# The closing norm of the last 256 rows, partly on the matmul array: one decoder layer step on one Trainium2 core

## The chip, the core and the metric

The kernel runs on one core of a Trainium2 chip, in one launch. The metric is the device time of one execution in microseconds; before the change it is 1931.59 us (the median of three runs, 1929.88 to 1933.46). Engines are named as in the profile: PE is the matmul engine (its weight loads are shown as PEld), DVE the vector engine, ACT the scalar engine, POOL the fourth compute engine, and SP the queue that issues nearly all DMAs here.

## The reference, cut to what matters

One layer of a hybrid decoder is computed in fp32 for 512 prompt rows (with 16 learned rows ahead of them) and 8 sample rows. The change lies in the last statement, the closing layer norm of the prompt rows:

```
def layer_norm(x, g, b):
    mu = jnp.mean(xf, -1, keepdims=True)
    var = jnp.mean(jnp.square(xf - mu), -1, keepdims=True)
    return (xf - mu) * lax.rsqrt(var + LN_EPS) * g + b
...
    ff = jnp.einsum('btf,fd->btd', a, w_down)
    return layer_norm(DEEPNORM_ALPHA * h1 + ff, ln2_g, ln2_b)
```

With r = 1/sqrt(var + eps), a row's result is r·(x·g) + (−mu·r)·g + b. The second form is the one that the changed kernel uses for six of its eight pieces.

## The kernel before

The trunk keeps features on partitions and tokens along the free axis. Each fp32 product is made of three fp32r matmuls: a weight is split into a high part (ACT, line 187) and a low part (DVE, line 188), the activations likewise, and `products` issues high·high (line 203), high·low (204) and low·high (206).

The end of the program is the part that matters. The down projection keeps 16 accumulators `acc[m]`, one for each 128 output features, over 520 token columns (8 sample, 512 prompt). Its last share, of four blocks of the inner dimension, is done by `down(h, m)`: for half h of the tokens (h = 0: the samples and prompt rows 0 to 255; h = 1: prompt rows 256 to 511) and block m, PE does four times three products of 256 columns into a bank of PSUM (the tiles `d0_m` and `d1_m`; `d` in the profile), and DVE adds the bank to `acc[m]` (line 1333). The weights are loaded by SP in four groups (line 1325) and split during h = 0; h = 1 uses the splits again.

The closing norm needs rows on partitions. So once four blocks of a half are added, PE transposes 128 rows by 512 features (tiles `tz8` and `tz136` for the first half, `tz264` and `tz392` for the second; line 1347), ACT copies them out of PSUM to a tile `z` (line 1349), and DVE takes statistics (line 1351). When all four quarters of a row block are there, `Rows.end` makes mean and reciprocal deviation by a chain of tiny operations (lines 236 to 250) and passes twice over each 512-wide quarter: centre and scale by the weight row (line 1358), then multiply by r and add the bias row (line 1360), and SP writes the quarter out (line 1361). Two row blocks make eight quarters, hence sixteen DVE passes of 128x512. Those of the first half are handed out piecewise among the products of h = 1 by the generator `ends`; those of the second half come after all products.

`sample_rows` does the same norm for the eight sample rows with features on partitions, in steps that the loop calls in turn (lines 1391 to 1408, the last of them a transposition `to` and sixteen small writes).

The order on each engine is set by a scheduler that places instructions by its own estimate of times; within an engine they run strictly in that order, and each waits on semaphores of other engines. `step(engine)` pins a written order.

## Time and profile before

| | |
|---|---|
| runs shown | 1933.46, 1929.88, 1931.59 us; median 1931.59 |
| profiled execution: span from first to last instruction | 1931.1 us |
| PE busy over the span | 1894.4 us (98%) |
| DVE busy | 1539.9 us (80%) |
| ACT busy | 944.1 us (49%) |
| span after the last product of the down projection (issued at 1911.33) | 19.8 us |

The page's span leaves out what lies ahead of the first and behind the last instruction; it stands 0.5 us below the median of the runs shown. In timeline rows the first number is the start in us, the second the time that the group of instructions covers, then engine, source line, operation, output and inputs, shape and count; a bracket gives idle time before the group and who ended it. In a table of windows each engine has busy time and the number of instructions, and PEclk is the granted clock of PE (1.00 is full). Successive DVE or PE instructions overlap slightly in these rows, so a cost is taken from start to start.

### The profile page before, as it was taken

The numbers are of one execution on the slowest core, as the hardware profiler recorded it, in microseconds if no ns is written. First come the engines' busy times: TensorE is split into PE (matmuls) and PEld (weight loads), VectorE is DVE, ScalarE is ACT, GpSimd is POOL, SyncE is SP. The second block draws the span as 40 slices with busy tenths as digits, with TensorE's granted clock in tenths as the row PEclk, the third lists the DMA queues.
The fourth block names the chain that finished last, engine by engine and source line by source line (L and its number), as shares of the span: only waits on it lengthen the run. The fifth ranks groups of instructions, "written<-read, shape, count | busy, mean of one in ns | idle before, by whom it ended". The sixth has DMA issues, their size and how long they took to land.

```text
span 1931.1 us, 39334 instructions
## 1 busy us (share of the span) xinstructions
PE 1894.4 (98%) x15533; PEld 1865.8 (97%) x15533; DVE 1539.9 (80%) x2734; ACT 944.1 (49%) x1808; POOL 2.7 (0%) x9
## 2 busy tenths in 40 slices
PE   9999999999999999999999999999999999999996
PEld 8999999999989999999999999999999999999996
DVE  6666667768777888888888888888877888888878
ACT  6644445545654544554455555555554444344341
POOL 0000000000000000000000000000000000000000
PEclk9999999999999999999999999999999999999998
DMA  8732222665744555454545445454469664645332
GB/s 276 233 101 66 71 78 75 211 202 193 250 150 164 160 160 172 142 162 158 175 139 178 141 138 165 146 167 145 164 212 356 214 221 162 223 163 202 94 99 89
DMA packets 145241, 319.28 MB, mean 165 GB/s; under 512 B 14288, under 2 KB 66232, under 8 KB 144952
## 3 DMA queue, kind: packets, MB, share of 16 engines
q1 hardware_dynamic: 144480, 315.71, 49.7%
q8 instruction: 122, 2.00, 0.4%
q10 hardware_dynamic: 576, 1.05, 0.2%
q14 instruction: 63, 0.52, 0.1%
HBM read 265.22 MB, written 54.03 MB: 165 GB/s over the span
## 4 chain that ended last, share of the span: by engine, by line
PE 92%; DVE 4%; ACT 2%; DMA 1%; issue 1%; SPq 0%; DVEq 0%; ACTq 0%
PE p_g L203 7%; PE p_g L204 7%; PE p_g L206 7%; PE p_u L203 7%; PE p_u L206 7%; PE p_u L204 7%; PE tri L203 7%; PE tri L206 7%; PE tri L204 7%; PE o L203 3%; PE o L206 3%; PE o L204 3%; PE p_u L996 2%; PE mm_u L203 2%; PE mm_u L206 2%; PE mm_u L204 2%
## 5 line engine op out<-in xcount | busy, mean ns | idle before, releaser
L187 ACT CAST rr<-fr 128x512 fp32r<-128x512 f32 (+1 forms) x1056 | 658.0, 643 | 776.6 <-DVE fr L196 224.0
L188 DVE TENSOR_TENSOR rr<-fr,rr 128x512 fp32r<-128x512 f32 (+1 forms) x1056 | 738.0, 717 | 264.5 <-ACT rr L187 253.2
L196 DVE TENSOR_TENSOR fr<-fr 128x1024 f32<-128x1024 f32 (+1 forms) x304 | 319.7, 1052 | 5.8 <-DMA fr<-in_w_g_dram 5.0
L203 PE MATMUL p_g<-rr 128*128 128x260 f32 x830 | 235.5, 285 | 7.4 <-ACT rr L187 7.1
L206 PE MATMUL p_g<-rr 128*128 128x260 f32 x830 | 230.6, 282 | 0.0
L204 PE MATMUL p_g<-rr 128*128 128x260 f32 x788 | 221.8, 282 | 0.0
L203 PE MATMUL p_u<-rr 128*128 128x260 f32 x770 | 217.5, 283 | 0.2 <-ACT rr L187 0.2
L206 PE MATMUL p_u<-rr 128*128 128x260 f32 x770 | 215.3, 282 | 0.0
L204 PE MATMUL p_u<-rr 128*128 128x260 f32 x748 | 210.6, 282 | 0.0
L206 PE MATMUL tri<-rr 128*128 128x260 f32 x696 | 196.8, 283 | 1.5 <-DVE rr L188 1.5
L203 PE MATMUL tri<-rr 128*128 128x260 f32 x696 | 197.0, 283 | 0.7 <-ACT rr L187 0.7
L204 PE MATMUL tri<-rr 128*128 128x260 f32 x696 | 196.7, 283 | 0.0
L203 PEld LDWEIGHTS p_g<-rr 128*128 128x128 f32 x830 | 156.2, 188 | 9.9 <-ACT rr L187 9.4
L206 PEld LDWEIGHTS p_g<-rr 128*128 128x128 f32 x830 | 155.2, 189 | 0.0
L204 PEld LDWEIGHTS p_g<-rr 128*128 128x128 f32 x788 | 148.1, 188 | 0.0
L203 PE MATMUL o<-rr 128*128 128x260 f32 x512 | 145.0, 284 | 0.3 <-ACT rr L187 0.3
L203 PEld LDWEIGHTS p_u<-rr 128*128 128x128 f32 x770 | 144.9, 188 | 0.3 <-ACT rr L187 0.3
L206 PEld LDWEIGHTS p_u<-rr 128*128 128x128 f32 x770 | 144.6, 189 | 0.0
L204 PE MATMUL o<-rr 128*128 128x260 f32 x512 | 144.1, 282 | 0.0
L206 PE MATMUL o<-rr 128*128 128x260 f32 x512 | 143.6, 282 | 0.2 <-DVE rr L188 0.2
L204 PEld LDWEIGHTS p_u<-rr 128*128 128x128 f32 x748 | 140.6, 188 | 0.0
L206 PEld LDWEIGHTS tri<-rr 128*128 128x128 f32 x696 | 131.3, 189 | 2.2 <-DVE rr L188 2.2
(320 smaller groups left out, 4570.0 us busy)
## 6 DMA issues: line engine op xcount, KB each, us to landing
fr<-in_w_u_dram SPq DMA_DIRECT2D x100, 512.0 KB
fr<-in_w_g_dram SPq DMA_DIRECT2D x90, 512.0 KB
fr<-in_w_d_dram SPq DMA_DIRECT2D x64, 640.0 KB
t_d<-fr SPq DMA_DIRECT2D x140, 260.0 KB
fr<-in_w_o_dram SPq DMA_DIRECT2D x64, 512.0 KB
fr<-in_w_in_dram SPq DMA_DIRECT2D x48, 512.0 KB
rr<-t_d SPq DMA_DIRECT2D x87, 260.0 KB
mid_b<-t_d SPq DMA_DIRECT2D x53, 260.0 KB
```

The lines of the kernel that those rows point to most:

```text
L187: nc.scalar.copy(wh, s)
L188: last_lo[0] = (lo or nc.vector).tensor_sub(wl, s, wh.bitcast(F32)).ins
L196: i = op(*args).ins
L203: nc.tensor.matmul(o, wh, hi[j], start=first, stop=False, skip_group_check=onto)
L204: nc.tensor.matmul(o, wh, lo[j], start=False, stop=False, skip_group_check=onto)
L206: nc.tensor.matmul(o, wl, hi[j], start=False, stop=last, skip_group_check=onto)
L996: nc.tensor.matmul(bk, self.q(0, n - 1)[:, k * P:(k + 1) * P], z1[0][4 * (n - 1) + k // 2][:, k % 2, :], start=(k == 0), stop=(k == 7))
```

## The change

Lines after 1333 shift (the bank add becomes line 1335; `Rows.end` has 1360 and 1362). Four things change, all in the second half's norm and what stands around it.

First, the rows 256 to 511 are no longer `Rows` but a class `Last`. Its `turn(m-1)` transposes one block for both row blocks inside `down(1, m)`, after three quarters of its products; before, the transpositions of four blocks stood together behind every fourth `down`. Each full quarter of the first three is copied out and measured as before, and DVE then multiplies it by the weight row at once (`scale`, line 1434), before the mean is known.

Second, the fourth quarter stays in PSUM. Its statistics are taken in two pieces of 256 columns (line 1426); after the last one, DVE centres and scales it straight from PSUM (line 1450) and finishes it as before (line 1457).

Third, for the other six pieces (three quarters, two row blocks) the terms (−mu·r)·g + b are made by PE: three columns −mu·r and two of ones (tile `five`) are transposed (line 1480), split into a high and a low part (`lh`, `lw`), and multiplied with five prepared rows that hold the weight and bias in high and low parts (`rows5`), 512 columns at a time into a bank `sh` (line 1501). For three pieces DVE adds r times the scaled tile to the bank (line 1507). For the three others PE also multiplies the scaled tile by a diagonal matrix of r, in fp32 (line 1496; the diagonals are made by ACT, line 1484), and ACT copies the bank out (line 1504).

Fourth, `rows5` is prepared during h = 0: four times two small loads by SP, a rounding copy by ACT (line 1536) and a DVE pass of 5x512 (line 1537). The steps of `sample_rows` move to behind blocks 3, 7 and 11 of the second half, where they were behind 4, 10 and 15.

```diff
-    def down(h, m):
+    def down(h, m, mid=None):
 ...
         for f in range(4):
             products([out], wh[:, f, :], wl[:, f, :], [ah[f][:, hs]], [al_[f][:, hs]], f == 0, f == 3)
+            if f == 2 and mid:
+                mid()
         nc.vector.tensor_add(acc[m][:, hs], acc[m][:, hs], out)
 ...
+        def turn(self, m):
+            q, i = divmod(m, 4)
+            if i == 0:
+                self.tp = bank(f"tz{self.c0}_{q}", 512)
+            nc.tensor.transpose(self.tp[:, i * P:(i + 1) * P], acc[m][:, self.c0:self.c0 + P], ident)
+            if q == 3:
+                if i % 2:
+                    nc.vector.bn_stats(self.st[:, 3 + i // 2, :], self.tp[:, (i - 1) * P:(i + 1) * P])
+            elif i == 3:
+                z = zp.tile([P, 512], F32, tag="z", name=f"z{self.c0}_{q}", bufs=NZ)
+                nc.scalar.copy(z, self.tp)
+                nc.vector.bn_stats(self.st[:, q, :], z)
+                self.z.append(z)
+        def scale(self, q):
+            nc.vector.tensor_mul(self.z[q], self.z[q], gb[0][q])
 ...
+        def centre(x):
+            dve.scalar_tensor_tensor(zl[x.i], x.tp, mu[:, x.i:x.i + 1], gb[0][3], op0=ALU.subtract, op1=ALU.mult)
 ...
+        affine(part[0])
+        with step(dve):
+            dve.scalar_tensor_tensor(five[:, :, 0:3], wide(mu), -1.0, wide(r), op0=ALU.mult, op1=ALU.mult)
+        with step(dve):
+            centre(part[1])
+        affine(part[1])
 ...
+        def diag(n):
+            x, q = pieces[n]
+            with step(nc.tensor):
+                nc.tensor.matmul(bk[n], dg[x.i], x.z[q], start=True, stop=False, skip_group_check=True)
+        def shift(n):
+            x, q = pieces[n]
+            with step(nc.tensor):
+                nc.tensor.matmul(bk[n], lw[:, x.i * P:(x.i + 1) * P], rows5[:, q * 512:(q + 1) * 512], start=n > 2,
+                                 stop=True, skip_group_check=True)
+            if n < 3:
+                nc.scalar.copy(x.z[q], bk[n])
+            else:
+                with step(dve):
+                    dve.scalar_tensor_tensor(x.z[q], x.z[q], r[:, x.i:x.i + 1], bk[n], op0=ALU.mult, op1=ALU.add)
+            put_out(x, q, x.z[q])
+        diag(0)
+        diag(1)
+        for n in (3, 4, 5, 0, 1):
+            shift(n)
+        diag(2)
+        shift(2)
 ...
+        if m in (6, 8, 10, 12):
+            affine_rows(m // 2 - 3)
 ...
+    ends = chain.from_iterable([x.end() for x in rows])
+    for m in range(KT):
+        down(1, m, lambda: [x.turn(m - 1) for x in last if m])
+        for _ in range(2 if m % 4 == 1 else 1):
+            next(ends, None)
+        if m % 4 == 2 and m > 2:
+            for x in last:
+                x.scale(m // 4 - 1)
+        if m in (3, 7, 11):
+            next(sample)
```

Where the instructions end up is shown at three places. In the names, `d1_m` is the bank of block m in the second half, `tz264_q` and `tz392_q` the transposed quarters q of its two row blocks, `mid_c` holds the tiles z, and `fr` the accumulators and the rows of weight and bias.

On DVE, in the middle of the second half, around the eight bias passes of the first half's rows; before:

```order
L242 TENSOR_TENSOR fr_60<-fr_60 128x1 x2
L1360 SCALAR_TENSOR_TENSOR mid_c_20115<-mid_c_20115,fr_60 128x512 x5
L1333 TENSOR_TENSOR fr_60<-fr_60,d1_9_20659 128x256
L1360 SCALAR_TENSOR_TENSOR mid_c_20115<-mid_c_20115,fr_60 128x512 x3
L1351 BN_STATS fr_60<-mid_c_20115 128x6 x2
L1333 TENSOR_TENSOR fr_60<-fr_60,d1_10_20676 128x256
```

and now:

```order
L1434 TENSOR_TENSOR mid_c_20115<-mid_c_20115,fr_60 128x512
L242 TENSOR_TENSOR fr_60<-fr_60 128x1 x2
L1335 TENSOR_TENSOR fr_60<-fr_60,d1_7_20641 128x256
L1393 TENSOR_REDUCE fr_60<-zv_20659 128x8
L1362 SCALAR_TENSOR_TENSOR mid_c_20115<-mid_c_20115,fr_60 128x512 x8
L236 TENSOR_SCALAR fr_60<-fr_60 128x8
L1335 TENSOR_TENSOR fr_60<-fr_60,d1_8_20672 128x256
L1335 TENSOR_TENSOR fr_60<-fr_60,d1_9_20693 128x256
L1430 BN_STATS fr_60<-mid_c_20115 128x6 x2
```

The eight passes now stand in one piece, and the adds of blocks 8 and 9 behind them; before, block 8 was added ahead of them and block 9 between them.

On PE, where the third quarter of the second half is first transposed; before:

```order
L204 MATMUL d1_11_20705<-rr_61 128x256
L206 MATMUL d1_11_20705<-rr_61 128x256
L1347 MATMUL tz264_2_20720<-fr_60 128x128
L1347 MATMUL tz392_2_20727<-fr_60 128x128
L203 MATMUL d1_12_20770<-rr_61 128x256
```

and now:

```order
L204 MATMUL d1_9_20693<-rr_61 128x256
L206 MATMUL d1_9_20693<-rr_61 128x256
L1423 MATMUL tz264_1_20603<-fr_60 128x128
L1423 MATMUL tz392_1_20605<-fr_60 128x128
L1423 MATMUL tz264_2_20703<-fr_60 128x128
L1423 MATMUL tz392_2_20705<-fr_60 128x128
L203 MATMUL d1_10_20714<-rr_61 128x256
```

The pair that reads block 8 stood behind the products of block 11 and stands now behind those of block 9.

At the end, PE had only the transposition `to` left after the last transpositions of the rows; it now has

```order
L1423 MATMUL tz392_3_20804<-fr_60 128x128
L1480 MATMUL five_20866<-fr_60 5x128 x2
L1496 MATMUL sh0_0_20873<-mid_c_20115,fr_60 128x512
L1496 MATMUL sh1_0_20874<-mid_c_20115,fr_60 128x512
L1501 MATMUL sh1_1_20876<-rr_61 128x512
L1501 MATMUL sh0_2_20877<-rr_61 128x512
L1501 MATMUL sh1_2_20878<-rr_61 128x512
L1501 MATMUL sh0_0_20873<-rr_61 128x512
L1501 MATMUL sh1_0_20874<-rr_61 128x512
L1496 MATMUL sh0_1_20875<-mid_c_20115,fr_60 128x512
L1501 MATMUL sh0_1_20875<-rr_61 128x512
```

so two of the three diagonal products stand ahead of all the rank products, and the third behind five of them; `sh0` and `sh1` are the two row blocks.

More of the change, by code (lines that the diff above doesn't have):

```diff
@@ L49 @@
 NG = 56
-NZ = 19
+NZ = 16
 FRW, RRW, MDW = 18960, 24368, 9880
@@ L1409, in sample_rows, with __init__ @@
         yield
+    class Last:
+        def __init__(self, c0, i, dst):
+            self.c0, self.i, self.dst, self.z = c0, i, dst, []
+            self.st = pb.tile([P, 5, 6], F32, name=f"st_z{c0}")
+        def turn(self, m):
[13 more added lines that the diff above has]
+            nc.vector.tensor_mul(self.z[q], self.z[q], gb[0][q])
@@ L1411, in hybrid_step @@
     sample = sample_rows()
     next(sample)
-    rows = [Rows(NS + P * i, P, yp[P * i:P * (i + 1), :]) for i in range(4)]
-    for h, part in ((0, rows[:2]), (1, rows[2:])):
-        for m in range(KT):
-            down(h, m)
-            if h == 1:
-                for _ in range(2 if m % 4 == 1 else 1):
-                    next(ends, None)
-            if h == 0 and m in (1, 2):
-                for i, q in gb_loads[4 * m - 4:4 * m]:
-                    nc.sync.dma_start(gb[i][q], ln2gb[i:i + 1, q * 512:(q + 1) * 512].to_broadcast([P, 512]))
-            if m % 4 == 3:
-                for x in part:
-                    x.part(m // 4)
-            if (h, m) in ((0, 4), (0, KT - 1), (1, 4), (1, 10), (1, KT - 1)):
-                next(sample)
-        ends = chain.from_iterable([x.end() for x in part])
@@ L1430, in hybrid_step @@
-    for _ in ends:
-        pass
+    five = pb.tile([P, 2, 5], F32, name="five")
+    nc.gpsimd.memset(five, 1.0)
+    nident = pb.tile([P, 8], F32, name="nident")
+    nc.scalar.activation(nident, ident[:, 0:8], AF.Copy, scale=-1.0)
+    mask = pb.tile([P, 1], F32, name="mask")
+    nc.vector.tensor_add(mask, nident[:, 1:2], nident[:, 4:5])
+    lp = Pool(rr)
+    lh = lp.tile([5, 2 * P], F32R, name="lh")
+    lw = lp.tile([5, 2 * P], F32R, name="lw")
+    rows5 = lp.tile([5, D], F32R, name="rows5")
@@ new lines, in affine_rows @@
+    def affine_rows(q):
+        sl = slice(q * 512, (q + 1) * 512)
+        g5 = pb.tile([5, 512], F32, name="g5", bufs=1)
+        h5 = lp.tile([5, 512], F32R, name="h5", bufs=1)
+        nc.sync.dma_start(g5[0:3], ln2gb[0:1, sl].to_broadcast([3, 512]))
+        nc.sync.dma_start(g5[3:5], ln2gb[1:2, sl].to_broadcast([2, 512]))
+        nc.scalar.copy(h5, g5)
+        nc.vector.scalar_tensor_tensor(rows5[:, sl], h5.bitcast(F32), mask[:5], g5, op0=ALU.mult, op1=ALU.add)
+    rows = [Rows(NS + P * i, P, yp[P * i:P * (i + 1), :]) for i in range(2)]
@@ new lines, in hybrid_step @@
+    last = [Last(NS + P * i, i - 2, yp[P * i:P * (i + 1), :]) for i in (2, 3)]
+    for m in range(KT):
+        down(0, m)
+        if m in (1, 2):
+            for i, q in gb_loads[4 * m - 4:4 * m]:
+                nc.sync.dma_start(gb[i][q], ln2gb[i:i + 1, q * 512:(q + 1) * 512].to_broadcast([P, 512]))
+        if m in (6, 8, 10, 12):
+            affine_rows(m // 2 - 3)
+        if m % 4 == 3:
+            for x in rows:
+                x.part(m // 4)
+        if m in (4, KT - 1):
+            next(sample)
@@ L1435, in _layout @@
+    ends = chain.from_iterable([x.end() for x in rows])
+    for m in range(KT):
+        down(1, m, lambda: [x.turn(m - 1) for x in last if m])
[5 more added lines that the diff above has]
+        if m in (3, 7, 11):
+            next(sample)
+    for _ in chain(ends, sample):
+        pass
+    for x in last:
+        x.turn(KT - 1)
+    last_rows(last)
 def _layout(i):
```

40 lines of the change are left out of this document (added).

## The prediction

> **What bounds the kernel now.** I looked first at where the end is decided, with a table of windows over the last 45 us (PE, PEld, DVE, ACT and POOL busy, each with its count, then clock, DMA share and GB/s).
>
> ```profile
> 1886.00:1891.00 5.00, 5.00 (x46) 5.00 (x45) 2.54 (x7) 2.36 (x3) 0.00 (x0) 1.00 0.00 0
> 1891.00:1896.40 5.40, 5.40 (x49) 5.40 (x48) 5.40 (x12) 0.41 (x2) 0.00 (x0) 1.00 0.01 3
> 1896.40:1901.00 4.60, 4.60 (x42) 4.60 (x41) 4.40 (x22) 1.28 (x3) 0.00 (x0) 1.00 0.01 2
> 1901.00:1906.60 5.60, 5.60 (x50) 5.60 (x49) 5.60 (x10) 1.07 (x2) 0.00 (x0) 1.00 0.72 256
> 1906.60:1912.60 6.00, 6.00 (x53) 5.87 (x52) 4.47 (x16) 1.05 (x3) 0.00 (x0) 1.00 0.32 114
> 1912.60:1922.00 9.40, 0.56 (x2) 0.18 (x1) 9.40 (x30) 1.89 (x6) 0.00 (x0) 0.65 0.03 6
> 1922.00:1931.10 9.10, 0.00 (x0) 0.00 (x0) 5.38 (x9) 0.00 (x0) 0.00 (x0) 0.50 0.64 231
> ```
>
> Up to 1912.6 PE is full and never waits; after it DVE alone works. But DVE is just as full between 1891 and 1906.6, so "under PE" there is not free. Next the timelines of DVE and PE, with the two sets of eight passes of the first half's rows, the last bank add, and the sixteen passes of the tail:
>
> ```profile
> 1891.04 2.73 DVE L1358 SCALAR_TENSOR_TENSOR mid_c<-mid_c,fr 128x512 f32<-128x512 f32 x4
> 1893.75 2.73 DVE L1358 SCALAR_TENSOR_TENSOR mid_c<-mid_c,fr 128x512 f32<-128x512 f32 x4
> 1896.47 0.73 DVE L1333 TENSOR_TENSOR fr<-fr,d 128x256 f32<-128x256 f32 x2
> 1900.98 3.40 DVE L1360 SCALAR_TENSOR_TENSOR mid_c<-mid_c,fr 128x512 f32<-128x512 f32 x5
> 1904.29 0.42 DVE L1333 TENSOR_TENSOR fr<-fr,d 128x256 f32<-128x256 f32 x1
> 1904.62 2.07 DVE L1360 SCALAR_TENSOR_TENSOR mid_c<-mid_c,fr 128x512 f32<-128x512 f32 x3
> 1906.61 1.28 DVE L1351 BATCH_NORM_STATS2 fr<-mid_c 128x6 f32<-128x512 f32 x2
> 1911.65 0.42 DVE L1333 TENSOR_TENSOR fr<-fr,d 128x256 f32<-128x256 f32 x1 [0.89 <-PE d L206]
> 1912.18 0.17 DVE L241 TENSOR_SCALAR fr<-fr 128x8 f32<-128x8 f32 x1
> 1915.05 0.28 DVE L1399 TENSOR_TENSOR fr<-fr 128x128 f32<-128x128 f32 x1
> 1915.25 0.38 DVE L250 BATCH_NORM_AGGREGATE fr<-fr 128x2 f32<-128x24 f32 x2
> 1915.74 2.73 DVE L1358 SCALAR_TENSOR_TENSOR mid_c<-mid_c,fr 128x512 f32<-128x512 f32 x4
> 1922.00 5.38 DVE L1360 SCALAR_TENSOR_TENSOR mid_c<-mid_c,fr 128x512 f32<-128x512 f32 x8
> ...
> 1885.41 0.36 PE L203 MATMUL d<-rr 128*128 128x256 f32 x1
> 1894.25 0.28 PE L203 MATMUL d<-rr 128*128 128x256 f32 x1
> 1894.37 0.28 PE L204 MATMUL d<-rr 128*128 128x256 f32 x1
> 1911.33 0.28 PE L206 MATMUL d<-rr 128*128 128x256 f32 x1
> 1911.45 1.25 PE L1347 MATMUL tz<-fr 128*128 128x128 f32 x10
> ```
>
> Prices from start to start: a pass 0.66 us (3.40 for five, less the overlap), statistics of 512 columns 0.60, a bank add 0.33, an operation of 128x128 about 0.2, a tiny one 0.07, or 0.19 when it needs the one ahead; a product 0.118, a transposition 0.108. The last product is done at 1911.6, the last pass at 1927.4. The writes then take 3.7 us to the end of the span; SP is not late, its last issues end with the passes. The share of the 16 queues' rate is the other limit there (a slice row of the DMA view over 1895 to 1932):
>
> ```profile
> 1925.60 2.14 SPq L1361 DMA_DIRECT2D out_dram<-mid_c  x4
> ...
> GB/s 0 0 0 0 0 9 0 0 292 383 343 365 328 365 166 29 22 0 0 0 0 0 0 0 9 13 13 11 11 4 15 385 326 379 357 376 385 53 0 0
> ```
>
> At about 370 GB/s a write of 256 KB takes 0.71 us.
>
> **The change, part by part.** *The tail's passes.* Sixteen passes (10.6 us) leave it; two centring, two finishing and three rank-sum passes (4.6 us) come in. Removed outright are three passes; six move, as multiplications of 0.60 (3.6 us), into the stretch ahead of the last product, where DVE has hardly any room. That much alone would be a gain.
>
> *The transpositions move forward, and make PE wait for DVE.* The order shows it: PE now needs the add of block m−1 inside the products of block m, and DVE still does the adds of blocks 3 and 4 behind the first eight passes and those of 8 and 9 behind the second eight. PE runs in order, so everything behind such a pair is held.
>
> First hold: from the first product at 1885.4, PE does 72 products (8.5 us), eight transpositions (0.9) and the sample's product (0.2) and stands at 1895.0 at the pair of block 3. The add of block 3 is done when it is before, at 1896.9; that of block 4, after a reduction, at 1897.4. PE goes on at 1897.5: 2.3 us lost, in two parts.
>
> Second hold: PE has 48 products, ten transpositions and one sample product to go, 7.0 us, and stands at 1904.3 (it gave back 0.2 by then) at the pair of block 8. DVE from 1897.3 has three adds (1.0), two statistics (1.2), two multiplications by the weight (1.2), two sample operations (0.4) and eight tiny ones (0.6), until 1901.7; then eight passes, 5.3 us, a tiny one, and the add of block 8, done at 1907.5. Lost: 3.3 us. Before, the same eight passes stood there too, but no transposition behind them was due until block 11.
>
> Third: until the add of block 10 DVE has 1 add, two statistics, two multiplications and four small operations of the sample norm, 3.5 us, and PE only 24 products and three pairs; about 0.4 us lost. The transposition `to` then waits for three dependent operations of 128x128: 0.8 us. After this PE needs 5.7 us for four blocks and DVE catches up. The four holds sum to 6.8 us, and some three pairs of transpositions that stood behind the last product now stand ahead of it (0.3 to 0.6). The last product is done at about 1918.8 instead of 1911.6: +7.2.
>
> *The tail from there.* Add and last transpositions to 1919.7, half-width statistics 2 x 0.30, aggregates and the tiny operation to 1920.9, centring 1921.6 (the square root on ACT beneath it), five dependent tiny ones 1922.5, finishing 1923.2, `five` 1923.3, the other centring and finishing 1924.7. PE starts its transpositions at 1923.4, the diagonals have been ready by then, and the first diagonal product starts at 1923.65. For its price the nearest row is fp32 work with 260 columns, where a product is two records (four products make the eight):
>
> ```profile
> 534.01 1.91 PE L996 MATMUL p_g<-fr 128*128 128x260 f32 x8
> ```
>
> 0.219 us a record, so 2 x 0.43 = 0.86 for 512 columns; a rank product is the fp32r kind, 0.24. That is at full clock. In series: two diagonals, five rank products, a diagonal, a rank product: 4.0 us. Which clock holds is told by other windows:
>
> ```profile
> 48.31:51.72 3.41, 1.91 (x11) 1.14 (x11) 1.05 (x5) 2.76 (x5) 0.00 (x0) 1.00 0.19 71
> 51.72:55.13 3.41, 3.41 (x15) 3.41 (x16) 2.92 (x5) 2.32 (x5) 0.00 (x0) 0.50 0.33 112
> 55.13:58.50 3.37, 3.37 (x30) 3.37 (x29) 2.74 (x7) 3.37 (x8) 0.00 (x0) 1.00 0.85 244
> ...
> 1911.98:1915.40 3.42, 0.73 (x7) 0.49 (x5) 3.36 (x11) 1.83 (x4) 0.00 (x0) 1.00 0.00 0
> 1915.40:1918.81 3.41, 0.45 (x1) 0.18 (x1) 3.41 (x10) 0.67 (x3) 0.00 (x0) 0.50 0.02 5
> ```
>
> The clock goes by windows of 3.41 us: one with 1.5 us of idle time is followed by one at half clock, in which full work makes 15 products instead of 30. PE idles 3.7 us ahead of `five`, so the diagonals start at half clock and the series takes up to 8 us. At half clock the first bank is ready at 1927.9, DVE's three passes end at 1929.9, and the last copy by ACT (0.6) at 1932.6; with the 3.7 us of the write the span ends at 1936.3. At full clock the copies end at 1928.5, but the six last writes come within 2 us and drain one by one: 1926.5 + 3.7 + 5 x 0.71 = 1933.7. One or two windows at half clock are nearest to the row, which is most of the difference: I take 1935.9, that is +4.8 against 1931.1 (+7.2 for the later last product, −2.4 in the tail).
>
> *The holds also cool PE.* The second hold puts at least 1.6 us of idle time into one window, by the rows above enough for a half-clock window, worth up to 1.7 us of products, part of it hidden by the third hold. Bounds 0 and 2.5; I take 0.6, since DVE is late anyhow. The sum is +5.4 on the profiled execution, and I put the same difference on the median, which is 0.5 us above its span: 1937.0.
>
> [...]
>
> *The preparation during h = 0.* Four DVE passes (2.6 us), four ACT copies (2.1) and eight small loads, which SP issues between the weight loads. The cover is this:
>
> ```profile
> 1862.16 5.74 SPq L1325 DMA_DIRECT2D fr<-in_w_d_dram  x8
> 1868.86 2.19 ACT L187 CAST rr<-fr 128x512 fp32r<-128x512 f32 x4 [3.14 <-DMA fr<-in_w_d_dram]
> 1869.52 0.69 DVE L188 TENSOR_TENSOR rr<-fr,rr 128x512 fp32r<-128x512 f32 x1 [3.90 <-ACT rr L187]
> 1871.73 0.37 PE L203 MATMUL d<-rr 128*128 128x264 f32 x1
> ```
>
> DVE and ACT idle there for over 3 us, and the split is ready 1.5 us before PE uses it. The third small load waits on SP for the second pass of 5x512 on DVE, right behind the splits that the weight loads wait for anyway, so it holds them by well under 1 us: nothing, unless it exceeds 1.5.
>
> **Rivals.** [...] *PE is not held*, because the adds come early enough: the last product is done at 1912.2, and the tail of 15 to 17.5 us gives 1927.8 to 1930.2. This decides once the holds sum to less than the 2 to 4.5 us that the tail gains. For it: PE waited for DVE for nothing before its last product; against it: 5.3 us of passes stand ahead of the adds in both orders, and only the transposition pair moved. *Both holds cool PE for two windows*: products stay slow until the third hold, some 3.4 us more, 1940 to 1943.
>
> **How the numbers follow.** A change within 0.2% (3.9 us) is about what a measurement of this kernel can tell from none. The forecast, 1934.7 to 1940, has 0.62 (0.56 of it slower, 0.06 the same); the full clock 0.12 (0.10 the same, 0.02 slower); PE not held 0.16 (half faster, half the same); the double cooling 0.10 (slower). That makes faster 0.08, same 0.24, slower 0.68. The range is 1930.0 to 1940.2: it leaves out the fast half of the unheld case (0.08) and the double cooling (0.10).
>
> **What would show it.** In the profile after: PE waiting for the bank add of line 1335 at transpositions of line 1423 near 1895 (2 us) and 1904 (3 us), in the table of waits; the last product near 1919; PEclk of 0.50 over the diagonal products of line 1496, with records of 0.8 us or more from start to start; the last write issued by 1933 or so. If PE shows no wait at 1904, the forecast is wrong at its main step; if the last product is near 1919 but the end is at 1933 or earlier, the tail's clock is.

## The result: 1.0038 times the time before, and where the profile shows it

The changed kernel takes 1939.02 us (median of five runs, 1938.27 to 1939.74) against 1931.59 before; the ratio is 1.0038, with a 95% interval of 1.0028 to 1.0049, so the change costs 5.4 to 9.5 us. The forecast was 1937.0 (1930.0 to 1940.2), slower with a chance of 0.68.

The profiled execution has a span of 1937.0 us and a time of 1938.91. Three stretches tell the most: from the first product of the first half to the first of the second (there the new preparation lies), from there to the last product, and from the last product to the end. The columns are those of the prediction's table of windows. Before:

```profile
1855.25:1885.41 30.16, 30.16 (x252) 29.95 (x250) 20.65 (x40) 12.12 (x28) 0.00 (x0) 1.00 0.39 114
1885.41:1911.33 25.92, 25.92 (x224) 25.92 (x223) 21.79 (x58) 5.54 (x12) 0.00 (x0) 1.00 0.23 83
1911.33:1931.07 19.74, 1.82 (x14) 1.32 (x12) 15.67 (x41) 2.73 (x7) 0.00 (x0) 0.60 0.31 110
```

and after, with four of the prediction's windows behind them:

```profile
1856.57:1886.41 29.84, 29.84 (x251) 29.84 (x250) 22.75 (x44) 14.47 (x32) 0.00 (x0) 1.00 0.39 117
1886.41:1919.63 33.22, 27.74 (x231) 26.65 (x230) 27.57 (x72) 6.88 (x15) 0.00 (x0) 1.00 0.19 66
1919.63:1937.01 17.38, 7.69 (x21) 3.21 (x19) 8.53 (x23) 2.92 (x7) 0.00 (x0) 0.84 0.34 121
1891.00:1896.40 5.40, 5.40 (x47) 5.25 (x45) 5.40 (x13) 1.04 (x3) 0.00 (x0) 1.00 0.01 3
1896.40:1901.00 4.60, 2.96 (x24) 2.67 (x24) 4.60 (x16) 1.28 (x3) 0.00 (x0) 1.00 0.01 2
1901.00:1906.60 5.60, 4.52 (x39) 4.28 (x38) 5.60 (x15) 1.07 (x2) 0.00 (x0) 1.00 0.38 141
1906.60:1912.60 6.00, 3.85 (x30) 3.49 (x30) 5.87 (x17) 0.21 (x1) 0.00 (x0) 1.00 0.60 220
```

The preparation costs nothing: 29.84 us against 30.16, and 29.84 to 29.89 in all ten kernels here that have it, 30.16 to 30.25 in the four without. The tail is 2.4 us shorter (17.38 against 19.74). The stretch between is 7.3 us longer (33.22 against 25.92): PE, which had not a gap in it, now idles 5.48 of it and works 1.82 longer. The last four windows show the other side: DVE is busy throughout, PE is not. PE's timeline has the idle times in brackets, and then the tail's series:

```profile
1898.00 0.97 PE L1423 MATMUL tz<-fr 128*128 128x128 f32 x4 [1.55 <-DVE fr L1335]
1908.71 0.41 PE L1423 MATMUL tz<-fr 128*128 128x128 f32 x2 [3.19 <-DVE fr L1335]
1913.27 0.33 PE L1405 MATMUL to<-fr 128*128 128x128 f32 x1 [0.61 <-DVE fr L1402]
1919.63 0.28 PE L206 MATMUL d<-rr 128*128 128x256 f32 x1
1925.08 0.58 PE L1480 MATMUL five<-fr 128*5 128x128 f32 x2 [3.76 <-DVE fr L1473]
1925.46 3.10 PE L1496 MATMUL sh<-mid_c,fr 128*128 128x512 f32 x4
1928.49 1.43 PE L1501 MATMUL sh<-rr 5*128 5x512 f32 x5
1929.84 1.12 PE L1496 MATMUL sh<-mid_c,fr 128*128 128x512 f32 x2
1930.90 0.50 PE L1501 MATMUL sh<-rr 5*128 5x512 f32 x1
```

The three waits are 5.35 us. The first row hides some 0.3 us more: two of its four transpositions need the add of block 4, and the four stand for 0.72 us from start to start (the next product is at 1898.72), where four in the kernel before stood for 0.35 (1898.14 to 1898.49). DVE's timeline shows why the second is the long one, and where DVE first waits for PE again, in the last blocks; its last row is the tail's three adds from the banks:

```profile
1902.78 5.38 DVE L1362 SCALAR_TENSOR_TENSOR mid_c<-mid_c,fr 128x512 f32<-128x512 f32 x8
1908.15 0.75 DVE L1335 TENSOR_TENSOR fr<-fr,d 128x256 f32<-128x256 f32 x2
1915.05 0.42 DVE L1335 TENSOR_TENSOR fr<-fr,d 128x256 f32<-128x256 f32 x1 [1.50 <-PE d L206]
1929.02 2.06 DVE L1507 SCALAR_TENSOR_TENSOR mid_c<-mid_c,fr,sh 128x512 f32<-128x512 f32 x3 [2.26 <-PE sh L1501]
```

PE's extra 1.8 us of work are mostly transpositions that stood behind the last product before. All work on the `tz` tiles between first and last product, before and then after (PE, PEld, DVE, ACT):

```profile
1885.41:1911.33 25.92, 5.04 (x29) 3.14 (x27) 1.39 (x2) 3.23 (x6) 1.00 0.23 83
```

```profile
1886.41:1919.63 33.22, 6.49 (x35) 3.73 (x33) 1.39 (x2) 4.30 (x8) 1.00 0.19 66
```

That is 1.45 us of busy time, the hidden 0.3 included; `to` with its 0.33 nearly makes up the rest. Busy times overlap with those of the products beside them, so this split is rough. In the tail, the three windows of the clock are the one before the diagonal products, the one over them, and the next:

```profile
1921.06:1924.47 3.41, 0.26 (x2) 0.02 (x1) 3.01 (x12) 0.57 (x3) 0.00 (x0) 1.00 0.00 0
1924.47:1927.89 3.42, 2.81 (x5) 1.33 (x6) 2.26 (x5) 0.70 (x3) 0.00 (x0) 0.50 0.39 147
1927.89:1931.30 3.41, 3.41 (x10) 1.32 (x8) 2.06 (x3) 1.07 (x2) 0.00 (x0) 1.00 0.21 79
```

One window is at half clock; it covers the first 2.4 of the 3.03 us that two diagonals take (1925.46 to 1928.49). What sets the end is a slice row of the DMA view over 1923 to 1937 (0.35 us a slice): two pieces pass alone, then nothing moves until the last six come together, and from 1930.7 the queues are full for 11 slices (0.9 or more of the 16 DMA engines' time, at 351 to 398 GB/s).

```profile
GB/s 0 0 0 0 0 0 0 47 380 322 0 0 310 380 59 0 0 0 0 0 0 59 392 363 398 369 375 357 351 369 357 386 363 234 99 23 0 0 0 0
```

Six writes of 0.71 us, as the prediction has them, end at about 1935, and the span 2 us later.

### The profile page after: what moved, and what is told of

The parts are those of the page before. It is cut to its first block, busy times and chain, and to the rows that moved or that the text cites. A ratio compares the mean times of both kernels' runs of the same rounds, so it can differ in the third digit from the quotient of the medians.

```text
span 1937.0 us, 39388 instructions
## 1 busy us (share of the span) xinstructions
PE 1902.3 (98%) x15547; PEld 1866.8 (96%) x15547; DVE 1540.3 (80%) x2734; ACT 947.5 (49%) x1816; POOL 2.8 (0%) x10
## 3 DMA queue, kind: packets, MB, share of 16 engines
q10 hardware_dynamic: 576, 1.05, 0.2%
## 4 chain that ended last, share of the span: by engine, by line
PE 92%; DVE 4%; ACT 2%; DMA 1%; issue 1%; SPq 0%; ACTq 0%; DVEq 0%
PE p_g L203 8%; PE p_g L204 8%; PE p_g L206 7%; PE p_u L203 7%; PE p_u L206 7%; PE p_u L204 7%; PE tri L203 6%; PE tri L206 6%; PE tri L204 6%; PE o L203 3%; PE o L206 3%; PE o L204 3%; PE p_u L996 2%; PE mm_u L203 2%; PE mm_u L206 2%; PE mm_q L203 2%
```

## The experiments

The theories, as the expectations name or use them. *Holds*: the loss is PE's waiting for DVE at the early transpositions. Two readings of it compete. *Order*: the bank adds stand behind eight passes, so another order would free PE. *Load*: DVE has more work before the last product than PE leaves room for (27.57 us of it instead of 21.79: 3.6 are the six multiplications, the rest came forward with the transpositions, statistics above all), so only less work or a later need frees PE. The rivals outside it: the *tail* (diagonal products and copies at half clock eat the gain), and on the clock *activity* (half clock behind a window of 3.41 us in which PE streams little, as the prediction's rows with 1.91 and 0.73 us of work have it) against *chance* (the clock falls by chance of where the edges of these windows lie, or not at all through idling).

All runs in one table, worked out from windows like those above: the stretch from first to last product, PE's mean granted clock and its idle time in it, the tail, all of one profiled execution; then the median and the ratio to the kernel before, run on the same chip (its medians there were 1931.17 to 1932.09).

| kernel | stretch | clock | PE idle | tail | median us | ratio (95%) |
|---|---|---|---|---|---|---|
| before | 25.92 | 1.00 | 0 | 19.74 | 1931.59 | |
| after | 33.22 | 1.00 | 5.48 | 17.38 | 1939.02 | 1.0038 (1.0028 to 1.0049) |
| turn4 | 38.15 | 0.87 | 7.73 | 18.22 | 1942.46 | 1.0055 (1.0042 to 1.0067) |
| before_mid | 30.77 | 1.00 | 3.37 | 18.62 | 1935.94 | 1.0025 (1.0015 to 1.0036) |
| pin | 35.87 | 0.90 | 5.24 | 18.55 | 1939.94 | 1.0043 (1.0031 to 1.0056) |
| dve6 | 36.11 | 0.86 | 4.64 | 16.49 | 1935.14 | 1.0021 (1.0011 to 1.0030) |
| noscale | 32.35 | 0.95 | 3.31 | 17.82 | 1935.06 | 1.0015 (1.0006 to 1.0023) |
| pool | 34.20 | 0.95 | 4.75 | 17.51 | 1937.62 | 1.0030 (1.0019 to 1.0042) |
| lag | 29.69 | 1.00 | 2.08 | 17.45 | 1932.58 | 1.0004 (0.9996 to 1.0013) |
| lag_pool | 29.58 | 1.00 | 1.93 | 16.88 | 1931.99 | 0.9998 (0.9989 to 1.0006) |
| warm_p | 34.99 | 0.90 | 4.66 | 16.32 | 1938.76 (one run) | |
| warm_t | 33.34 | 0.95 | 4.83 | 16.37 | 1937.27 (one run) | |
| tail_pe | 27.55 | 1.00 | 0.66 | 18.43 | 1931.14 | 0.9996 (0.9987 to 1.0005) |
| tail_pe2 | 27.17 | 1.00 | 0.25 | 16.93 | 1930.32 | 0.9992 (0.9983 to 1.0001) |

A mean clock of 0.95 is one window of 3.41 us at half clock, 0.90 two, 0.87 and 0.86 three. At the granted 0.50 one can cost at most half its length, 1.7 us, of the stretch (18 records stand in noscale's and 18 and 19 in dve6's, against 30 at full clock in the prediction's row from 55.13), so stretches of different clock can't be compared as they stand. The idle time is smaller where the clock was lower: 4.64 to 4.83 us in dve6, warm_p and warm_t against 5.48 in after, with the same order. That slower products leave DVE more time is the author's estimate from this. Nine kernels of the table have the early turns (after to pool, warm_p and warm_t). In seven of their profiled executions the stretch has such windows; only those of after and before_mid have none.

**The early transpositions alone (before_mid).** The kernel before, with one thing of the change: the transpositions of block m−1 stand inside the products of block m, and nothing else.

```diff
...
-            down(h, m)
+            down(h, m, (lambda: [x.turn(m - 1) for x in part if m]) if h else None)
...
-                    x.part(m // 4)
+                    if h == 0:
+                        x.part(m // 4)
+                    elif m == KT - 1:
+                        x.turn(m)
```

> The kernel before with that one part alone: each block's pair of transpositions of the second half's rows inside the products of the next block; tail, multiplications and everything else as before. Holds theory: the array waits 4 to 6 us for bank adds, the last product comes that much later, and the tail of sixteen passes is as long as it was, so 1935.5 to 1938. Rival 1 (the tail costs): 1931 to 1932. Rival 2 (the early multiplications fill the vector engine): they are not here, so at most 2 us of waiting, 1932 to 1933.5.

Measured 1.0025, 1935.94. Its first-to-last stretch and its waits in the table of waits (total, times, longest):

```profile
1883.42:1914.19 30.77, 27.40 (x231) 26.63 (x229) 24.77 (x66) 6.61 (x14) 0.00 (x0) 1.00 0.20 70
```

```profile
PE tz L1360 <- DVE fr L1335: 3.6, 4, 1.5
```

With the tail untouched but for the 1.1 us that move ahead, the transpositions cost 4.85 us of stretch, 3.37 of it idle time of PE and 1.48 more work. The waits are fewer than the 4 to 6 us expected, the time is in the range of the holds theory. So the holds are the larger part of the loss, and the multiplications by the weight are not needed for them: 3.0 us more DVE work than before (24.77 against 21.79) came forward with the transpositions alone. With the rest of the change it is 5.8 us more, and PE idles 5.48.

**Turns in fours (turn4).** The changed kernel with the transpositions of the first three quarters written four together behind blocks 3, 7 and 11, to have them at three places rather than twelve.

```diff
-        down(1, m, lambda: [x.turn(m - 1) for x in last if m])
+        down(1, m, lambda: [x.turn(m - 1) for x in last if m > 12])
+        if m in (3, 7, 11):
+            for x in last:
+                for i in range(m - 3, m + 1):
+                    x.turn(i)
```

> The changed kernel with one part undone: the transpositions of the first three quarters stand four together behind blocks 3, 7 and 11 again (the last quarter stays inside the products). Holds theory: the array stood 5 to 7 us for bank adds that came behind passes; here the last product is issued at about 1913 instead of 1919.6, the array waits under 1 us for adds, and the time is 6 to 7 us below the changed kernel's: 1932.3 (1931 to 1934). Rival 1, the tail is what costs (half clock, writes): the end moves by less than 1 us, 1938 to 1939. Rival 2, the vector engine simply has too much work in this stretch because of the six early multiplications (3.6 us): the last product stays at 1916 to 1918 whatever the order, 1936 to 1938.

This was a miss: 1.0055, the slowest of all. The place in the text is not the place on the engine: the scheduler put the turns between products again, ahead of late adds, and the wait at `to` grew from 0.61 to 2.87 us:

```profile
1910.05 0.69 PE L1423 MATMUL tz<-fr 128*128 128x128 f32 x2 [2.54 <-DVE fr L1335]
1913.61 0.45 PE L1405 MATMUL to<-fr 128*128 128x128 f32 x1 [2.87 <-DVE fr L1402]
```

Three windows of its stretch are at half clock besides (mean clock 0.87; its products stand 0.21 us apart from 1914.07 to 1918.76, and 0.12 behind 1919.54). What it was to test did not come about, so it decides nothing between the theories.

**Written order on DVE (pin).** The changed kernel, with the adds and the passes of the first half's rows pinned in the written order, so that no more than two passes stand ahead of an add.

```diff
-        nc.vector.tensor_add(acc[m][:, hs], acc[m][:, hs], out)
+        if h:
+            with step(nc.vector):
+                nc.vector.tensor_add(acc[m][:, hs], acc[m][:, hs], out)
+        else:
+            nc.vector.tensor_add(acc[m][:, hs], acc[m][:, hs], out)
...
-            next(ends, None)
+            with step(nc.vector):
+                next(ends, None)
```

> The changed kernel with the vector engine's bank adds of the second half and the sixteen passes of the first half's rows held in written order, one or two passes between two adds instead of eight; the same work. Holds theory: no add has more than two passes ahead of it, the waits of the array sum to under 2 us, the last product is issued at 1914 to 1915, time 1933.5 to 1935.5. Rival 2 (too much work on the vector engine, not its order): the last product stays at 1918 or later, time 1937.5 to 1939.5. Rival 1 (tail): 1938 to 1939.

1.0043, within the intervals of the changed kernel. Its waits:

```profile
PE tz L1427 <- DVE fr L1337: 4.6, 6, 1.2
PE to L1409 <- DVE fr L1406: 0.6, 1, 0.6
```

4.6 us, as the 4.7 in two pieces in the changed kernel (1.55 and 3.19), only in six. Two windows of the stretch are at half clock (its mean is 0.90); with at most 3.4 us for them taken off, it would still be over 32 us, where 28 or so was expected if the order were the cause. So the order theory falls: this order deals out the waiting in another way, and its sum is the same.

**Less work on DVE (noscale).** The six multiplications by the weight row are left out (so the six pieces lack their weight); they are 3.6 us of DVE work and nothing else hangs on them.

```diff
-            nc.vector.tensor_mul(self.z[q], self.z[q], gb[0][q])
+            pass
```

> The changed kernel without the six early multiplications by the weight row (six pieces come out unweighted); everything else and the order of the passes as it was. Load theory (the vector engine has no room ahead of the last product, so the array is held by the amount of its work and not by which pass stands where): without these 3.6 us the time from the first to the last product of the second half, 33.2 us in the changed kernel, falls to 30.3 to 31.3, the value of the kernel before with early transpositions alone (30.8), and the time to 1935 to 1937.5. Order theory (eight passes in one piece stand ahead of the adds): the stretch stays at 32.5 to 34, time 1938 to 1939.7.

1.0015, 1935.06. The stretch contains one window at half clock:

```profile
1905.50:1908.90 3.40, 3.40 (x18) 3.40 (x18) 2.81 (x11) 0.68 (x3) 0.00 (x0) 0.51 0.21 78
```

Its 18 records against some 30 at full clock cost about 1.4 us of the stretch of 32.35 (12 products of 0.118). Without it the stretch would be about 30.9, close to before_mid's 30.77, with as much DVE work in it (24.77 us, in both). This is the load theory: by this estimate 2.3 us of stretch for 3.6 us of work. The time bears it out, since the interval lies wholly below that of the changed kernel.

**The same work on POOL (pool).** The multiplications are given to the idle fourth engine.

```diff
-            nc.vector.tensor_mul(self.z[q], self.z[q], gb[0][q])
+            nc.gpsimd.tensor_mul(self.z[q], self.z[q], gb[0][q])
```

> The changed kernel with the six early multiplications moved from the vector engine to the idle fourth compute engine. Load theory, if that engine works beside the vector engine without slowing it: as without the multiplications, stretch 30.3 to 31.5, time 1935 to 1937.5. If the two hinder each other: passes of the vector engine of over 0.70 us from start to start while a multiplication runs, stretch over 32, time 1937.5 to 1940. Order theory: stretch 32.5 to 34 with passes of 0.66 us, 1938 to 1939.7.

1.0030: about a third of what leaving the work out brings, and the interval overlaps that of the changed kernel, so that even this third isn't shown. POOL's row, and a DVE operation beside it:

```profile
1909.51 2.53 POOL L1434 TENSOR_TENSOR mid_c<-mid_c,fr 128x512 f32<-128x512 f32 x2 [7.58 <-DVE fr L1430]
```

```profile
1910.16 0.66 DVE L239 TENSOR_TENSOR fr<-fr 128x8 f32<-128x8 f32 x1
1910.86 1.21 DVE L240 TENSOR_TENSOR fr<-fr 128x8 f32<-128x8 f32 x1
```

A multiplication takes 1.26 us on POOL against 0.60 on DVE, and a DVE operation of 128x8, 0.17 us in the changed kernel, stands for 1.21, until 1912.07, and POOL is through at 1912.04. What makes it wait is not shown.

**Later turns (lag, lag_pool).** If load decides, the way out is to need the adds later. Both kernels turn block m−3 inside block m (the last ones closer), with the order on PE pinned, and have six adds by DVE for the tail (as dve6 below); the sample's steps stand behind blocks 3, 8 and 15 in lag and behind 4, 10 and 15 in lag_pool, which also multiplies on POOL.

```diff
-        down(1, m, lambda: [x.turn(m - 1) for x in last if m])
+        down(1, m, lambda: [x.turn(i) for i in [[], [], [], [0], [1], [2], [3], [4], [5], [6], [7], [8], [9], [10, 11], [12, 13], [14]][m] for x in last])
...
-        if m in (3, 7, 11):
+        if m in (3, 8, 15):
```

> Transpositions three blocks behind the products that they read instead of one (kept there by pinning the array's order), the sample norm's steps at blocks 4, 10 and 15 or near as before, all six pieces by the vector engine; the multiplications stay on the vector engine. Load theory: an add may be up to three blocks late, so the vector engine's busy stretch is covered by products; waits for adds under 2 us ahead of block 12, stretch 28.5 to 30, tail 15 to 16.5, time 1929.5 to 1933. Order theory: the eights of passes are where they were, so stretch 32 or more, time 1935 or more.

> The same with the six multiplications on the fourth compute engine. Load theory: stretch 27 to 28.5 against 25.9 before, tail 14 to 16 against 19.7, the span 2 to 3.5 us shorter than before: 1927.5 to 1929.5, ratio 0.998 to 0.9995. If that engine slows the vector engine: no better than with the multiplications on the vector engine, 1930 to 1934. Order theory: 1934 or more.

lag is back at the time before, 1.0004 (0.9996 to 1.0013), lag_pool at 0.9998 (0.9989 to 1.0006); neither is told apart from it. The stretch and the tail of lag:

```profile
1883.16:1912.85 29.69, 27.61 (x232) 26.84 (x231) 26.93 (x70) 6.62 (x14) 0.00 (x0) 1.00 0.20 72
1912.85:1930.30 17.45, 4.70 (x14) 2.35 (x12) 10.61 (x29) 0.72 (x3) 0.00 (x0) 0.55 0.37 124
```

PE has 27.6 us of work there and DVE 26.9, and the stretch is 29.7, 3.5 below the changed kernel's, with nearly all the work still in it. The tail was expected at 15 to 16.5 and came out at 17.45; its gain of 2.3 us against the kernel before is less than the 3.8 us by which the stretch is longer (1.7 more work on PE, 2.1 of idle time). POOL brought nothing to the stretch (29.58): five passes take 4.39 us beside it (two multiplications run there from 1897.48 to 1900.02), against 3.40 in the prediction's row.

```profile
1898.82 4.39 DVE L1363 SCALAR_TENSOR_TENSOR mid_c<-mid_c,fr 128x512 f32<-128x512 f32 x5
```

**The tail without diagonals (dve6).** The changed kernel; diagonals and ACT's copies are gone, and DVE adds all six banks.

```diff
-            if n < 3:
-                nc.scalar.copy(x.z[q], bk[n])
-            else:
-                with step(dve):
-                    dve.scalar_tensor_tensor(x.z[q], x.z[q], r[:, x.i:x.i + 1], bk[n], op0=ALU.mult, op1=ALU.add)
+            with step(dve):
+                dve.scalar_tensor_tensor(x.z[q], x.z[q], r[:, x.i:x.i + 1], bk[n], op0=ALU.mult, op1=ALU.add)
...
-        diag(0)
-        diag(1)
-        for n in (3, 4, 5, 0, 1):
+        for n in range(6):
```

> The changed kernel without the diagonal products and the copies by the scalar engine: for all six pieces the array makes the rank product only and the vector engine adds r times the scaled tile. Theory from the trace after (the end is set by six writes that drain one by one behind the first finished piece, which stands at 1929.6 because the diagonals run first and at half clock): the first piece is done at 1927.6, the last at 1931, the span ends at 1934.9 instead of 1937.0, time 1936.9 (1936.2 to 1937.8); the last product stays at 1919.6. Rival, the diagonals save time since the array works beside the vector engine: six adds of 0.66 us in a row end later than three, and the time is 1939 to 1940.5.

The tail is 0.9 us shorter (16.49 against 17.38), where 2.1 was expected: the array's share of the pieces brought this tail nothing. The median, 1935.14, is below what was expected, by more than the tail explains; its ten runs reach from 1933.06 to 1938.57 and the profiled one took 1937.77, so the tail isn't the whole difference and the rest stays open. Part of that spread is seen in the profiled execution. The order up to the last product is that of the changed kernel, yet here three windows at half clock follow the holds, one behind the first and two behind the second:

```profile
1892.39:1895.80 3.41, 1.77 (x14) 1.33 (x14) 3.41 (x11) 0.45 (x1) 0.00 (x0) 1.00 0.00 0
1895.80:1899.21 3.41, 3.41 (x19) 3.41 (x18) 3.09 (x13) 0.83 (x3) 0.00 (x0) 0.50 0.01 2
1902.62:1906.04 3.42, 1.42 (x13) 1.17 (x11) 3.42 (x6) 1.07 (x2) 0.00 (x0) 1.00 0.96 351
1906.04:1909.45 3.41, 2.41 (x12) 2.44 (x13) 3.41 (x9) 0.21 (x1) 0.00 (x0) 0.50 0.72 266
1909.45:1912.86 3.41, 3.41 (x18) 3.41 (x17) 2.03 (x9) 0.00 (x0) 0.00 (x0) 0.50 0.00 0
```

where the changed kernel's corresponding window was followed by full clock:

```profile
1903.99:1907.41 3.42, 1.53 (x14) 1.29 (x12) 3.42 (x6) 1.07 (x2) 0.00 (x0) 1.00 0.87 318
1907.41:1910.82 3.41, 2.11 (x18) 2.14 (x19) 3.41 (x10) 0.21 (x1) 0.00 (x0) 1.00 0.80 299
```

Four executions have this same order up to the last product (after, dve6, warm_p, warm_t), with none, three, two and one windows at half clock in it, and their stretches are 33.22, 36.11, 34.99 and 33.34: cooling is worth 0 to 2.9 us for one and the same order. What decides between them no run shows.

**Keeping the array busy ahead of the diagonals (warm_p, warm_t).** The changed kernel, with 30 more products, or 32 more transpositions, on PE while it waits for `five`; their results aren't used. They and the last transpositions of the rows are held in written order on PE.

```diff
...
+            for _ in range(30):
+                nc.tensor.matmul(tt, ws[KT - 1][0][:, 0, :], ah[0][:, DHALF[1]], start=True, stop=True)
```

```diff
...
+            for _ in range(32):
+                nc.tensor.transpose(tt[:, 0:P], acc[KT - 1][:, NS + 2 * P:NS + 3 * P], ident)
```

> The changed kernel with 30 needless products of 256 columns on the array between the last transpositions of the rows and the transposition of the five columns, where it idled 4.4 us. Only the stretch behind the last product is read. Activity theory (a window of 3.41 us in which the array streams little is followed by half clock): clock 1.00 over the diagonals, the first two take 1.75 us instead of 3.0, the stretch from the last product to the end is 16.0 to 16.5 us instead of 17.4. Rival (the clock falls by chance of the grid or not at all through idling): 0.50 somewhere over the first two diagonals, 17 to 18.5.

> The same with 32 needless transpositions of 128 columns in place of the products. If any work of the array keeps its clock (as I read the rows of before): clock 1.00 over the diagonals, last product to end 16.0 to 16.5 us. If transpositions don't count as work for the clock: 0.50 over the first two diagonals as without them, 17 to 18.5 us.

Both had one run each, so the tail is the reading, not the time. warm_p's tail, and its two diagonals (four records):

```profile
1920.51:1936.83 16.32, 9.80 (x51) 6.19 (x49) 8.52 (x23) 2.93 (x7) 0.00 (x0) 0.88 0.39 129
```

```profile
1926.08 1.88 PE L1499 MATMUL sh<-mid_c,fr 128*128 128x512 f32 x4
```

The two diagonals take 1.81 us from start to start instead of 3.03 and the tail 16.32 instead of 17.38: the half clock cost the tail 1.1 us. With transpositions alone the clock holds just as well (1.00); warm_t's window of them and the next:

```profile
1920.91:1924.32 3.41, 3.28 (x30) 3.04 (x28) 3.20 (x14) 0.90 (x3) 0.00 (x0) 1.00 0.00 0
1924.32:1927.74 3.42, 3.39 (x12) 1.63 (x12) 2.59 (x5) 0.49 (x2) 0.00 (x0) 1.00 0.41 153
```

In this run, then, a window that held next to nothing but transpositions, 3.28 us of them, was followed by 1.00, where the changed kernel's with 0.26 us of work was followed by 0.50.

**What is left when the holds are gone (tail_pe, tail_pe2).** On the kernel before. In the second half the third quarter is transposed as one group inside block 13 and half of the fourth inside block 15; nothing is multiplied early. In the tail the fourth quarter is centred from PSUM, and three pieces (two in tail_pe2) are finished by PE, with a diagonal in fp32 and a product of one row for the bias, and copied out by ACT; 28 products stand ahead of them to keep the clock (1.00 from 1917.95 to 1921.37 in tail_pe, over the first diagonals). The sample's step behind block 10 moves to behind block 8 (9 in tail_pe2).

```diff
+        by_pe = (0, 1, 4)
...
+            if n in by_pe:
+                with step(nc.tensor):
+                    nc.tensor.matmul(bk[n], dg[i], z, start=True, stop=False, skip_group_check=True)
+                with step(nc.tensor):
+                    nc.tensor.matmul(bk[n], ones1, gb[1][q][0:1, :], start=False, stop=True,
+                                     skip_group_check=True)
+                nc.scalar.copy(z, bk[n])
...
-            down(h, m)
+            down(h, m, (lambda: [x.turn(i) for i in {13: (8, 9, 10, 11), 15: (12, 13)}.get(m, ()) for x in part]) if h else None)
```

```diff
-        by_pe = (0, 1, 4)
+        by_pe = (0, 1)
```

> A version made from the findings, on the kernel before: no early multiplications; the third quarter transposed inside the products of block 13 and half of the last one inside block 15, since the vector engine has room only there; the last quarter centred from PSUM; three of eight pieces finished by the array (diagonal of r in fp32, then the bias row by a rank-one fp32 product, copied out by the scalar engine), so thirteen vector passes instead of sixteen in the tail; 28 needless products keep the clock up before. Load theory: first to last product 26 to 28.5 us (25.9 before, 33.2 in the changed kernel), last product to end 15 to 16.5 (19.7 before), time 2 to 4 us below the kernel before: ratio 0.9978 to 0.9992. Rival (what makes the changed kernel slow is its tail with the diagonals): the tail stays at 18 or more, time 1931 to 1935.

tail_pe came to 0.9996 (0.9987 to 1.0005), a miss: 0.9978 to 0.9992 was expected. The stretch hardly grew (27.55, PE idle 0.66), but the tail took 18.43 us instead of 15 to 16.5, since the third piece of the array was late. The window with fp32 diagonals and one-row products is full, and the next is at half clock all the same:

```profile
1917.95:1921.37 3.42, 3.42 (x8) 0.88 (x6) 3.42 (x7) 0.59 (x1) 0.00 (x0) 1.00 0.32 118
1921.37:1924.78 3.41, 3.41 (x5) 1.00 (x4) 3.39 (x6) 0.58 (x1) 0.00 (x0) 0.50 0.74 271
```

and since its write, whose copy by ACT ends at 1926.29, stood at the head of SP's queue, three pieces that DVE had finished by 1924.76 waited behind it; SP's last row takes 4.52 us for four:

```profile
1923.12 4.52 SPq L1463 DMA_DIRECT2D out_dram<-mid_c  x4
```

Tail and time are those that the rival gave, so the next kernel takes the late piece out.

> As the version before it, but two of eight pieces by the array instead of three, and the sample norm's chain one block later. There the third piece came at half clock (4.1 us for its two products) and its write, at the head of SP's queue, held back three finished pieces: 18.4 us from the last product to the end. If that is what took the gain: fourteen vector passes end about 12.5 us after the last product, no write waits for the array, last product to end 16 to 17 us, first to last product 26.5 to 28, time 1.5 to 3 us below the kernel before: ratio 0.9983 to 0.9995. If the tail is bound otherwise (the drain of the writes, the sample's small writes): 18 us or more again, ratio 0.9993 to 1.0005.

With two pieces on the array the tail is 16.93:

```profile
1884.43:1911.60 27.17, 26.92 (x231) 26.55 (x229) 23.42 (x64) 6.50 (x14) 0.00 (x0) 1.00 0.22 79
1911.60:1928.53 16.93, 8.99 (x44) 5.06 (x42) 12.79 (x30) 2.34 (x6) 0.00 (x0) 0.77 0.35 128
```

It measures 1930.32, 0.9992 (0.9983 to 1.0001). Stretch and tail together are 44.10 us against 45.66 before and 50.60 after. It beats the changed kernel by far; against the kernel before, the interval still touches 1, and a gain isn't proven.

## Why the prediction held, point by point

**The first term, holds: +7.2 at the last product.** Measured +7.3 in the stretch (33.22 less 25.92), so the sum was right; its parts were not. The holds were sized 2.3, 3.3, 0.4 and 0.8, 6.8 together; they measured 1.55 (and the 0.3 hidden behind it), 3.19, none, and 0.61, that is 5.35 to 5.7. The work that moves ahead of the last product was sized 0.3 to 0.6 and measured 1.8 (1.45 busy on `tz`, the hidden 0.3 included, 0.33 for `to`). The two errors cancel, and that they do so to 0.1 us is luck.

**The cause given for the holds** was half wrong. The prediction put them down to eight passes standing ahead of the adds. pin has at most two there and waits as long; noscale, with 3.6 us less for DVE, has a stretch shorter by about 2.3 once its half-clock window is taken off, and lag, which needs the adds later, one shorter by 3.5. It is the amount of DVE's work before the need that counts. A sum over DVE's work up to each add, as the prediction made it, counts this whatever the story, though it came out over a microsecond too long here.

**The tail, −2.4.** Measured −2.4 (19.74 to 17.38), and one window at half clock over the diagonals, as forecast. The reason for the end was again another. By the forecast ACT's last copy and its write would be last. The last copy is done at 1932.0, and with 3.7 us for its write would give 1935.7; the trace has the queues full from 1930.7 on, and the end by that is 1929.7 (DVE's first add, 1929.02 + 0.69) + 3.7 + 5 x 0.71 = 1936.95, measured 1937.0. That is the formula that the prediction had for full clock. With the forecast's own times at half clock it gives 1935.8 (1927.9 + 0.66 + 3.7 + 5 x 0.71), near the 1936.3 that the copy gave, so the wrong reason cost little.

**Cooling of the holds, 0.6.** In the profiled execution it is 0, in the four of the same order 0 to 2.9, so the bounds (0 and 2.5) were nearly right and the single value tells little. That there is none in the changed kernel's own profile is an exception: seven of the nine profiles with early turns have one to three windows. The prediction's reading, that 1.5 us of idle time is enough, isn't a rule: the changed kernel's window with 1.53 us of work, and so 1.89 of idle time, was followed by full clock, dve6's with 1.77 and 1.42 of work by half. Half clock came behind windows with 13 and 14 records, full clock behind one with 14. The other traces are no clearer: before_mid's window with 1.90 us of work was followed by full clock, the kernel before's with 1.91 (the prediction's row) and noscale's with 1.73 (1902.20 to 1905.60) by half. What decides stays open.

**The preparation, 0.** Right, by the stretch of the first half in all fourteen profiles.

**The base.** The term that was mis-sized is what lies around the span. The prediction set the time before at the span plus 0.5, since the median of the runs stands there. In each of the thirteen profiles taken since, the time is its own span plus 1.8 to 2.1 (1938.91 for 1937.0). So the profiled execution before stood near 1933.0, 1.4 above the median shown, and 1931.1 + 5.4 + 1.9 gives 1938.4 against 1939.02 measured. On spans the sum was +5.4 and came out at +5.9: +7.3 −2.4, and +1.0 from the upstream work, whose end (the first product of the second half) is at 1885.41 before, 1886.41 after, and from 1882.47 to 1885.93 in the others. The difference is there at the first product of the first half already (1855.25, 1856.57), ahead of the preparation. So of the 7.4 us between the medians, the two stretches that this account explains hold 4.9; the other 2.5 are these +1.0 and the before profile's 1.4, neither traced to the change. Cooling may be part of it: over the whole span the changed kernel's other four runs were granted 0.992 or 0.993, the profiled one 0.996; where in the span, no run shows.

**The rivals.** *PE is not held*: excluded by the waits. *Full clock* (0.12): excluded in the tail by the 0.50 window; in the middle the clock did stay at 1.00 in this execution. Had it held in the tail too, the tail would have been 16.3 us (warm_p), not the 14.9 that the prediction's 1933.7 meant (1933.7 less 1918.8; 15.2 if counted from the issue of the last product, as in the table). *Double cooling*: not in this profile, but dve6's comes near it with one window behind the first hold and two behind the second, and its profiled run is the second slowest of ten.

## What to carry to other kernels

Before work is moved "under" a busy engine, sum what the other engine has to do before each point at which the busy one will need it: here DVE had been full there already. before_mid has 3.0 us more DVE work ahead of the last product and 3.4 us of idle time on PE, the changed kernel 5.8 and 5.5; lag, which needs the results later, has 5.1 and 2.1. The one other order that kept to its text (pin) dealt out such a shortage and did not lessen it; less work (3.31 us of idle time in noscale) or a later need (2.08 in lag) lessens it, and what remains of a tail's gain has to pay for it. At the end of a kernel look at the writes: once several pieces finish together, the queues' rate (351 to 398 GB/s over the last six writes here) and the order of the issuing queue (4.52 us for four writes in tail_pe) can set the end, not the compute.

## What the runs showed of the hardware

PE's clock fell to half behind a window of 3.41 us that was busy for 1.77 us (dve6), and also behind one that was busy throughout with fp32 products of 512 columns and of one row (tail_pe); it stayed full behind one busy for 1.53 us (after) and behind one with 30 transpositions of 128x128 (warm_t, one run). An fp32 product of 128x512 takes 0.90 us at full clock when two follow each other (1.81 for both, warm_p). With a one-row product behind it, one takes 1.05 us at full clock (1917.31 to 1918.36 in tail_pe) and 2.01 at half (1921.60 to 1923.61). A DVE operation of 128x8, 0.17 us in the changed kernel, stood for 1.21 us while POOL multiplied (pool, line 240).
